# Block products for the feed-forward's output projection, on one Trainium2 core

## The chip, the core and the metric

The kernel runs on one core of a Trainium2 chip, in one launch. The metric is the device time of one execution in microseconds (us). TensorE multiplies matrices into psum; VectorE (DVE), ScalarE (ACT) and GpSimd (POOL) work element by element; SyncE (SP) issues all the transfers that matter here. VectorE and ScalarE read psum, POOL works on SBUF tiles alone.

## What is computed

The reference is one layer of a decoder trunk on 1024 prompt rows and 8 sample rows: a feed-forward, a token-mixing block, cross-attention, a second feed-forward, each with a residual and a LayerNorm. The change concerns the two feed-forwards alone:

```python
D_MODEL, D_FF = 1024, 2816
DN_ALPHA = (2.0 * DEPTH) ** 0.25          # DEPTH = 1

def _swiglu(h, wi, wo):
    u = h @ wi
    gate, up = u[..., :D_FF], u[..., D_FF:]
    return (jax.nn.silu(gate) * up) @ wo

h = _layer_norm(DN_ALPHA * h + 0.5 * _swiglu(h, P['ffn1_wi'], P['ffn1_wo']), P['ln_g'][0], P['ln_b'][0])
...
h = _layer_norm(DN_ALPHA * h + 0.5 * _swiglu(h, P['ffn2_wi'], P['ffn2_wo']), P['ln_g'][3], P['ln_b'][3])
```

All values are float32.

## The kernel before

Activations lie transposed: channels on the 128 partitions, the NT = 1032 rows along the free dimension. `S.acc` holds the 8 channel tiles of the residual stream. Every matrix product takes both operands as a high part and a low part (`split`: ScalarE rounds the high part, VectorE subtracts it for the low one) and runs three matmuls per tile, high by high, high by low, low by high (`mm3`, L125 to L127). `S.HH` and `S.HL` hold the two parts of 8 tiles of activations.

A feed-forward (`ffn`) has two stages. In the first, the hidden values silu(gate) times up are made, 22 tiles of 128 channels. Two tiles go as plain products (`classic`), the other 20 as 10 pairs (`pair`), in which the gate projection and then the up projection of two tiles are each made as seven block products in Winograd's form of Strassen's scheme: `left` loads four blocks of weights into raw tiles, forms their sums on POOL (L334) and yields the seven left factors B11, B21, T1, B22, T2, T3, T4 in this order; the right factors were made at the start (`UpForms`). HN = NT/4 = 258 is the width of one block of columns, p = 0, 1 are the halves of the rows. The hidden values of a pair, `G[m][p]`, go to a DRAM tensor `HID` (L407).

In the second stage the 22 hidden tiles come back in eight groups (`groups`, `loads`): 258-KB loads of HID and 256-KB loads of `wo` into raw tiles, each split in two. For each group, each of 8 output blocks m and each of the three column ranges CH3 (344 columns), `down_tile` sums the group's products in psum; ScalarE writes the first group's result to `S.acc` (L440), VectorE adds the others (L442). The residual `src` is added to `S.acc` on POOL between the groups (L464). The last group goes range by range, with the sums that LayerNorm needs (`ln_stat_step`).

LayerNorm is a stream of 20 steps (`ln_stream`): mean (L169), subtraction (L181), squares (L183), their sums over the partitions (L176), a power on POOL (L193), transposes that spread it (L200), scaling (L205), bias (L207), and, where another block follows, the two parts in HH and HL. `weave` interleaves such streams step by step as the program is written, so that of several streams the one with the smallest share done goes next; a second entry of a pair says how many steps a stream counts as. `settled` holds a stream back until the norm of the columns that it needs has been written. Norms that are pending at the end of a block are woven into the start of the next one.

The program is written with a scheduling layer that sets the order on each engine when it is built; on the chip each engine runs its list in that order. psum tiles of the feed-forward come from 6 banks, in the first stage from 8; the norms have two of their own in the second. Raw tiles: 7. Pairs of weight tiles: 7 in the first stage.

Of the kernel before, what the change touches and what calls it, by code (L numbers as in the profile page):

```python
# [19 lines left out]
NT = NP + NS  # L20
# [115 lines left out]
def ln_stat_step(S, st, m, c0, n):  # L136
# [23 lines left out]
def ln_stream(S, st, li, c0, n, final, keep):  # L160
# [11 lines left out]
    adds = nc.gpsimd if final is None or c0 + n < NT else nc.vector  # L172
# [6 lines left out]
    for k in range(KT):  # L179
        d = acc[:, k, c0:c0 + n]  # L180
        nc.vector.tensor_tensor(out=d, in0=d, in1=mu[:, :n], op=ALU.subtract)  # L181
        sq.append(S.lnp.tile([128, S.lnw], F32, tag="lnq", name="lnq", bufs=3))
# [39 lines left out]
LN_STEPS = 20  # L222

# [59 lines left out]
def ffn(S, octx, wi, wo, li, src, pre=(), final=None, keep=None, after=None):  # L283
# [5 lines left out]

    nc, tc = S.nc, S.tc  # L290
    HID = S.dram.tile([JT, 128, NT], F32, name="HID%d" % li)
    with ExitStack() as ctx:
# [39 lines left out]
        gt = pool(uctx, "fg", 6)  # L332
        TT = lambda o, a, b, op: nc.vector.tensor_tensor(out=o, in0=a, in1=b, op=op)
# [30 lines left out]
        def pair(j):  # L364
# [46 lines left out]
        groups = [[0, 1]] + [[3 * g + i for i in (2, 3, 4)] for g in range(5)] + [[17, 18], [19, 20, 21]]  # L411
        hd, wt = {}, {}
        S.hlseq = itertools.cycle([S.whl] * 2 + [S.hlx] * 2)

        def loads(js, to=None):
            for j in js:
                hd[j] = to() if to else (S.HH[:, j % KT, :], S.HL[:, j % KT, :])
                for p in range(2):
                    N = slice(2 * HN * p, 2 * HN * p + 2 * HN)
                    x = raw_tile(S)  # L420
                    nc.sync.dma_start(out=x, in_=HID[j, :, N])
                    split(nc, [t[:, N] for t in hd[j]], x)
                wt[j] = load_split(S, wo[128 * j:128 * j + 128, :])

        loads(groups[0])
        uctx.close()
        S.norms = Norms(S, octx, 344)
        hlast = pool(ctx, "fhl", 3)
        xw = pool(ctx, "fwo", 5)
        S.hlseq = itertools.cycle([S.hlx] * 2 + [xw] * 2 + [S.whl] * 3 + [xw] * 3 + [S.hlx] * 2)  # L430

        def down_tile(js, m, ni, st=None):
            c0, n = CH3[ni]
            q = psum(n)
            for j in js:
                hh, hl = hd[j]
                mm3(nc, q, wblock(wt[j], m), hh[:, c0:c0 + n], hl[:, c0:c0 + n], j == js[0], j == js[-1])
            a = S.acc[:, m, c0:c0 + n]
            if js[0] == 0:
                nc.scalar.activation(out=a, in_=q, func=AF.Identity, scale=0.5 / ALPHA)  # L440
            else:
                nc.vector.scalar_tensor_tensor(out=a, in0=q, scalar=0.5 / ALPHA, in1=a, op0=ALU.mult, op1=ALU.add)  # L442
            if st is not None:
                ln_stat_step(S, st, m, c0, n)

        def down_last(js, ni, st):
            for m in range(KT):
                down_tile(js, m, ni, st)
                yield

        banks = itertools.cycle([ps])
        last = lambda: [hlast.tile([128, NT], F32R, tag="h" + x, name="h" + x) for x in "hl"]
        for g, js in enumerate(groups[:-1]):
            loads(groups[g + 1], last if g + 2 == len(groups) else None)
            for m in range(KT):
# [1287 lines left out]
```

## Time and profile before

| | us |
|---|---|
| median of 3 executions | 3201.08 (3195.89 to 3203.86) |
| the profiled execution | 3202.45 |
| its span in the profile | 3200.7 |
| TensorE busy | 3015.8 |
| VectorE busy | 2198.6 |
| ScalarE busy | 1434.0 |
| POOL busy | 558.1 |

An engine's busy time is the union of its instructions. The records of neighbouring matmuls overlap, so the time that one costs is read from how many start in a stretch, not from its record. A wait is put down to what came last by the profile. Of the stages, the first feed-forward lies between 0 and about 724 us, the token mixing and attention between that and about 2448 us, the second feed-forward behind.

### The profile page before, as it was taken

The page shows a single profiled execution, that of the slowest core. Times are in us where ns is not written, and L with a number is a line of the kernel's source. Part 1 is how long each engine was busy: PE and PEld are TensorE (multiplying, and loading weights), DVE is VectorE, ACT ScalarE, POOL GpSimd, SP SyncE. Part 2 cuts the span into 40 slices and gives each one's busy share as a digit, 9 for nine tenths or more (in the row PEclk, how much of TensorE's full clock was granted, in tenths as well). Part 3 has the DMA queues.
Part 4 walks back from the last instruction along what each step waited for, and adds up shares of the span by engine and source line. Part 5 has one row for each costly group of instructions (what it writes and reads, how often), then busy time and mean ns, then how long its engine had stood idle before and what let it go on. Part 6 is the DMA issues. An engine that isn't in the chain of part 4 may idle for free. (4 is left out here: it accounts for less than half of the span.)

```text
span 3200.7 us, 63254 instructions
## 1 busy us (share of the span) xinstructions
PE 3015.8 (94%) x23324; PEld 2848.3 (89%) x23324; DVE 2198.6 (69%) x5903; ACT 1434.0 (45%) x3195; POOL 558.1 (17%) x526
## 2 busy tenths in 40 slices
PE   8999999999999999999999979889897999999997
PEld 8999999999888888888878858778887999999997
DVE  7666665574366887777777877776678666666556
ACT  5333352125465565556455655364235433334212
POOL 2222200132010011010001000260005322220111
PEclk9999999999999999999998969899999999999998
DMA  4222253314644554545554455554543222225321
GB/s 138 80 80 78 79 162 107 111 48 140 205 126 132 148 145 137 137 126 155 138 146 115 129 140 153 172 181 128 153 120 125 71 80 80 80 80 159 107 86 54
DMA packets 391301, 386.72 MB, mean 121 GB/s; under 512 B 153904, under 2 KB 292176, under 8 KB 390992
## 3 DMA queue, kind: packets, MB, share of 16 engines
q1 hardware_dynamic: 390992, 382.69, 40.4%
q8 instruction: 183, 3.00, 0.4%
q14 instruction: 126, 1.03, 0.1%
HBM read 277.54 MB, written 105.23 MB: 120 GB/s over the span
## 5 line engine op out<-in xcount | busy, mean ns | idle before, releaser
L125 PE MATMUL ps<-HH,wh 128*128 128x258 f32 (+1 forms) x2384 | 718.6, 302 | 18.7 <-ACT HH L510 7.8
L126 PE MATMUL ps<-HL,wh 128*128 128x258 f32 (+1 forms) x2384 | 716.7, 301 | 0.0
L127 PE MATMUL ps<-HH,wl 128*128 128x258 f32 (+1 forms) x2384 | 715.7, 300 | 0.0
L125 PE MATMUL g<-HH,wh 128*128 128x344 f32 (+2 forms) x1840 | 624.5, 340 | 15.9 <-DVE ql L1435 4.2
L127 PE MATMUL g<-HH,wl 128*128 128x344 f32 (+2 forms) x1840 | 596.8, 325 | 1.0 <-DVE wl L100 1.0
L126 PE MATMUL g<-HL,wh 128*128 128x344 f32 (+2 forms) x1840 | 594.3, 324 | 0.6 <-POOL HL L215 0.4
L125 PEld LDWEIGHTS ps<-HH,wh 128*128 128x128 f32 x2384 | 451.4, 189 | 21.0 <-ACT HH L510 7.8
L126 PEld LDWEIGHTS ps<-HL,wh 128*128 128x128 f32 x2384 | 451.2, 189 | 0.4 <-DVE HL L511 0.3
L127 PEld LDWEIGHTS ps<-HH,wl 128*128 128x128 f32 x2384 | 450.4, 189 | 0.0
L125 PEld LDWEIGHTS g<-HH,wh 128*128 128x128 f32 x1840 | 357.1, 194 | 35.3 <-DVE ql L1435 5.5
L126 PEld LDWEIGHTS g<-HL,wh 128*128 128x128 f32 x1840 | 357.7, 195 | 5.3 <-POOL HL L215 1.4
L127 PEld LDWEIGHTS g<-HH,wl 128*128 128x128 f32 x1840 | 356.1, 194 | 5.1 <-DVE wl L100 1.3
L228 ACT ACTIVATE wh<-raw 128x512 fp32r<-128x512 f32 x280 | 176.4, 631 | 322.2 <-PE ps L126 262.7
L334 POOL TENSOR_TENSOR raw<-raw 128x512 f32<-128x512 f32 x160 | 214.0, 1337 | 566.6 <-DVE wl L229 383.2
L229 DVE TENSOR_TENSOR wl<-raw,wh 128x512 fp32r<-128x512 f32 x280 | 206.7, 739 | 138.6 <-ACT wh L228 131.8
L100 DVE TENSOR_TENSOR wl<-raw,wh 128x512 fp32r<-128x512 f32 x302 | 218.6, 731 | 100.6 <-ACT wh L99 98.3
L99 ACT ACTIVATE wh<-raw 128x512 fp32r<-128x512 f32 x302 | 184.6, 625 | 222.5 <-PE ps L126 76.0
L442 DVE SCALAR_TENSOR_TENSOR acc<-ps,acc 128x344 f32<-128x344 f32 x336 | 168.4, 512 | 141.1 <-PE ps L127 140.4
L551 DVE TENSOR_TENSOR pr<-tq,iv 128x2 f32<-128x2 f32 (+30 forms) x496 | 160.8, 324 | 3.2
L556 ACT ACTIVATE ev<-g 128x344 f32<-128x344 f32 x192 | 86.9, 453 | 136.8 <-PE g L127 132.0
L949 DVE TENSOR_REDUCE tq<-pr 128x1 f32<-128x2 f32 (+30 forms) x496 | 121.8, 246 | 2.9
L556 ACT ACT_TABLE_LOAD x93 | 119.3, 1283 | 6.9 <-DVE cs L551 2.9
(404 smaller groups left out, 6302.8 us busy)
## 6 DMA issues: line engine op xcount, KB each, us to landing
raw<-in_wi_dram SPq DMA_DIRECT2D x176, 256.0 KB, 2.9
raw<-in_w_in_dram SPq DMA_DIRECT2D x116, 256.0 KB, 3.2
GD<-ev SPq DMA_DIRECT2D x168, 172.0 KB, 1.9
raw<-in_wo_dram SPq DMA_DIRECT2D x104, 256.0 KB, 2.8
raw<-HID SPq DMA_DIRECT2D x88, 258.0 KB, 3.6
HID<-g SPq DMA_DIRECT2D x80, 258.0 KB, 2.3
tg<-GD SPq DMA_DIRECT2D x32, 512.0 KB, 4.0
wt<-T SPq DMA_DIRECT2D x160, 64.0 KB, 2.9
```

What stands on the lines that cost most here:

```text
L99: nc.scalar.activation(out=hi, in_=raw, func=AF.Identity)
L100: S.low.tensor_tensor(out=lo, in0=raw, in1=hi.bitcast(F32), op=ALU.subtract)
L125: nc.tensor.matmul(ps, wh, xh, start=first, stop=False)
L126: nc.tensor.matmul(ps, wh, xl, start=False, stop=False)
L127: nc.tensor.matmul(ps, wl, xh, start=False, stop=last)
L228: nc.scalar.activation(out=hi, in_=x, func=AF.Identity)
L229: nc.vector.tensor_tensor(out=lo, in0=x, in1=hi.bitcast(F32), op=ALU.subtract)
L334: pool_tt = lambda o, a, b, op: nc.gpsimd.tensor_tensor(out=o, in0=a, in1=b, op=op)
L442: nc.vector.scalar_tensor_tensor(out=a, in0=q, scalar=0.5 / ALPHA, in1=a, op0=ALU.mult, op1=ALU.add)
L551: TTo = lambda o, a, b, op: nc.vector.tensor_tensor(out=o, in0=a, in1=b, op=op)
L556: ACT = lambda o, a, f=AF.Identity, **kw: nc.scalar.activation(out=o, in_=a, func=f, **kw)
L949: nc.vector.tensor_reduce(out=tq[:, 0:m, i], in_=pv, axis=mybir.AxisListType.X, op=ALU.add)
```

## The change

The output projection is made as seven block products as well. The 22 hidden tiles are taken as 11 pairs, rows of the product's inner dimension, so that each pair gives blocks (b11, b12; b21, b22) of hidden values, 128 channels by 258 columns for each half p, and of `wo`, 128 channels by 512 output columns. For each of seven forms and each half p, four output blocks are summed in psum over all 11 pairs and then added to `S.acc`, with the signs and partial sums of the scheme.

- In the first stage each pair now also makes its sums of hidden blocks (`hidden`: four subtractions of 258 columns per half on POOL, seven blocks written to DRAM `HF`) and of `wo` blocks (`sums`: four loads, four operations on 512 columns on POOL, four stores to DRAM `WF`). The two tiles made as plain products go by way of HID into such a pair, number 0, behind the first of the others.
- In the second stage form f's hidden blocks are loaded and split (`hid_prep`), its weights likewise (`w_prep`). While half 0 of form f runs, the hidden blocks of form f+1 are prepared; while half 1 runs, its weights. HH and HL hold the blocks of one form in the columns of one kind (b·1) and of the next form in those of the other kind, with extra tiles for pairs 8 to 10. There are 13 pairs of weight tiles.
- `S.acc` is loaded with the residual itself, by DMA; the POOL additions of it go.
- The last two forms finish columns 258 to 516, 774 to 1032, 0 to 258 and 516 to 774 in this order, so LayerNorm runs in four ranges of 258 columns in place of three of 344. The last half product goes block by block.
- `first_of` counts a norm's 20 steps as 80 where it is handed on: between the feed-forward's last half products, into the token mixing, into attention and into the second feed-forward.

The core of the diff:

```diff
@@ ln_stat_step, ln_stream, Norms @@
-        st.s = S.lnp.tile([128, S.lnw], F32, tag="lns", name="lns")[:, :n]
+        st.s = S.lnp.tile([128, 264], F32, tag="lns", name="lns", bufs=S.lnsums)[:, :n]
...
-    adds = nc.gpsimd if final is None or c0 + n < NT else nc.vector
+    adds = nc.gpsimd if final is None or c0 != 2 * HN else nc.vector
...
+def first_of(norm):
+    return norm[0], 4 * norm[1]
@@ ffn, first stage @@
-            for m in range(2):
-                for p in range(2):
-                    nc.sync.dma_start(out=HID[j + m, :, 2 * HN * p:2 * HN * p + 2 * HN], in_=G[m][p])
+            hidden(j // 2, G)
+
+        def hidden(i, G):
+            T = [ft.tile([128, 2 * HN], F32, tag="t%d" % t, name="t%d" % t) for t in range(4)]
+            sub = lambda o, a, b: pool_tt(o, a, b, ALU.subtract)
+            for p in range(2):
+                (b11, b12), (b21, b22) = ((g[p][:, :HN], g[p][:, HN:]) for g in G)
+                N = slice(HN * p, HN * p + HN)
+                t1, t2, t3, t4 = (t[:, N] for t in T)
+                for f, b in ((0, b11), (1, b21), (3, b22)):
+                    nc.sync.dma_start(out=HF[i, f, :, N], in_=b)
+                sub(t1, b12, b11)
+                sub(t3, b22, b12)
+                sub(t2, b22, t1)
+                sub(t4, t2, b21)
+            for f, t in zip((2, 4, 5, 6), T):
+                nc.sync.dma_start(out=HF[i, f], in_=t)
...
+        def sums(i):
+            t = [ft.tile([128, 512], F32, tag="w%d" % x, name="w%d" % x) for x in range(5)]
+            for x, b in zip(t, ((0, 0), (0, 1), (1, 1), (1, 0))):
+                nc.sync.dma_start(out=x, in_=weight(i, *b))
+            a11, a21, a22, a12, s1 = t
+            pool_tt(s1, a21, a22, ALU.add)
+            pool_tt(a21, a11, a21, ALU.subtract)
+            pool_tt(a11, a22, a21, ALU.subtract)
+            pool_tt(a12, a12, a11, ALU.subtract)
+            for n, x in enumerate((s1, a11, a21, a12)):
+                nc.sync.dma_start(out=WF[i, n], in_=x)
@@ ffn, second stage: groups, loads, down_tile, down_last and the POOL additions go @@
+        def hid_prep(f, k):
+            x = raw_tile(S)
+            nc.sync.dma_start(out=x, in_=HF[k, f])
...
+            split(nc, to, x.rearrange("q (p n) -> q p n", p=2))
+            HX[f, k] = to
+
+        def w_prep(f, k):
+            src = (weight(k, 0, 0), weight(k, 1, 0), WF[k, 0], WF[k, 3], WF[k, 1], WF[k, 2], weight(k, 1, 1))[f]
+            x = raw_tile(S)[:, :512]
+            nc.sync.dma_start(out=x, in_=src)
...
+            split(nc, W[f, k], x)
+
+        def add(f, q, m, p):
...
+            onto = lambda o, s=sc: nc.vector.scalar_tensor_tensor(out=o, in0=q, scalar=s, in1=o, op0=ALU.mult,
+                                                                 op1=ALU.add)
+            if form == "B11":
+                nc.scalar.activation(out=u, in_=q, func=AF.Identity, scale=sc)
+                pool_tt(c11, c11, u, ALU.add)
+            elif form == "B21":
+                onto(c11)
+            elif form == "T1":
+                onto(c12)
+                onto(c22)
+            elif form == "B22":
+                onto(c12)
+            elif form == "T2":
+                onto(u)
+                pool_tt(c12, c12, u, ALU.add)
+            elif form == "T3":
+                onto(u)
+                TT(c22, c22, u, ALU.add)
+                pool_tt(c21, c21, u, ALU.add)
+            else:
+                onto(c21, -sc)
+
+        def one_pass(f, p, st=None):
...
+            qs = [psum(HN) for _ in range(4)]
+            for k in range(NJ):
+                if f < 6:
+                    (w_prep if p else hid_prep)(f + 1, k)
+                for m in range(4):
+                    step(m, k, qs[m])
+                yield
+            for m in range(4):
+                result(m, qs[m])
+
+        for k in range(KT):
+            hid_prep(0, k)
+            if k < 7:
+                w_prep(0, k)
         uctx.close()
...
+        for k in range(KT):
+            nc.sync.dma_start(out=S.acc[:, k, :], in_=src[k])
+        pre = []
+        for f, p in itertools.product(range(7), range(2)):
+            st = SimpleNamespace() if f > 4 else None
+            weave((one_pass(f, p, st), NJ), *pre)
+            if (f, p) == (6, 0) and after is not None:
+                ahead(S, after)
             if st is not None:
+                pre = [first_of((ln_finish(S, st, li, 2 * HN * p + HN * (6 - f), HN, final, keep), LN_STEPS))]
     return pre
@@ mixer, attention @@
-        return [norm(3)]
+        return [first_of(norm(3))]
```

## Rows read from the trace of the kernel before

**Rows 1.** The page's first part: busy time, share of the span, instructions.

```profile
PE 3015.8 (94%) x23324; PEld 2848.3 (89%) x23324; DVE 2198.6 (69%) x5903; ACT 1434.0 (45%) x3195; POOL 558.1 (17%) x526
```

**Rows 2.** Stretches: length, each engine's busy time (instructions), granted clock, DMA share, GB/s.

```profile
57.00:460.00 403.00, 403.00 (x3361) 403.00 (x3360) 272.91 (x511) 152.98 (x316) 101.46 (x76) 1.00 0.27 86
500.00:600.00 100.00, 100.00 (x635) 100.00 (x634) 59.25 (x106) 20.63 (x35) 10.86 (x8) 1.00 0.37 112
724.00:732.00 8.00, 4.80 (x15) 4.33 (x16) 6.08 (x16) 7.66 (x18) 6.14 (x7) 0.59 0.72 256
2467.00:2495.00 28.00, 20.76 (x114) 20.04 (x114) 20.45 (x40) 14.67 (x38) 16.02 (x17) 0.82 0.21 71
2510.00:2913.00 403.00, 403.00 (x3361) 403.00 (x3361) 270.53 (x502) 150.86 (x309) 100.41 (x76) 1.00 0.27 85
2913.00:3175.00 262.00, 258.14 (x1643) 256.04 (x1641) 155.59 (x294) 63.30 (x121) 33.37 (x29) 1.00 0.31 96
3175.00:3200.70 25.70, 8.54 (x32) 6.57 (x32) 15.52 (x35) 10.84 (x22) 0.85 (x1) 0.59 0.31 110
2900.00:2925.00 25.00, 23.17 (x174) 22.88 (x173) 19.84 (x41) 15.78 (x34) 0.00 (x0) 1.00 0.81 254
```

**Rows 3.** Matmuls of the tiles T4 and hh: durations ns, first and last start.

```profile
L127 PE MATMUL ps<-T4h,wl x8: 281/283/287, 457.2 to 459.8; 128*128 128x258 f32 x8
L127 PE MATMUL ps<-hh,wl x72: 313/320/406, 678.0 to 723.4; 128*128 128x344 f32 x72
L127 PE MATMUL ps<-T4h,wl x160: 281/283/287, 2527.7 to 2913.1; 128*128 128x258 f32 x160
L127 PE MATMUL ps<-hh,wl x72: 313/320/404, 3131.4 to 3174.0; 128*128 128x344 f32 x72
```

**Rows 4.** ScalarE's groups by line, 445 to 467 us: count, busy us, mean ns, idle.

```profile
L228 ACT ACTIVATE HH<-raw 128x516 fp32r<-128x516 f32 x12 | 7.4, 632 | 7.3 <-DMA raw<-HID 7.2
L99 ACT ACTIVATE wh<-raw 128x512 fp32r<-128x512 f32 x8 | 4.9, 625 | 3.5 <-issue 2.0 <-DMA raw<-in_wo_dram 1.5
```

**Rows 5.** Groups by line and shape, whole span: count, busy us, mean ns, idle.

```profile
L334 POOL TENSOR_TENSOR raw<-raw 128x512 f32<-128x512 f32 x160 | 214.0, 1337 | 566.6 <-DVE wl L229 383.2 <-DMA raw<-in_wi_dram 75.3 <-issue 56.5
L229 DVE TENSOR_TENSOR HL<-raw,HH 128x516 fp32r<-128x516 f32 x76 | 54.6, 734 | 34.6 <-ACT HH L228 34.5
L333 DVE TENSOR_TENSOR p<-p,ps 128x258 f32<-128x258 f32 x80 | 33.9, 424 | 46.4 <-PE ps L127 41.1
L181 DVE TENSOR_TENSOR acc<-acc,ln 128x344 f32<-128x344 f32 x48 | 22.4, 504 | 2.5 <-PE ln L169 2.3
L181 DVE TENSOR_TENSOR acc<-acc,ln 128x256 f32<-128x256 f32 x48 | 18.2, 411 | 1.2 <-PE ln L169 1.2
```

**Rows 6.** Instructions of LayerNorm in order of time: start us, duration us.

```profile
2434.34 0.59 PE L169 MATMUL ln<-lns,ones_d 128*128 128x256 f32 x2
2443.87 0.44 PE L200 MATMUL ln<-ident,lnx 128*128 128x128 f32 x2 [1.49 <-ACT lnx L195]
2450.34 1.08 PE L169 MATMUL ln<-lns,ones_d 128*128 128x264 f32 x2
2474.36 0.90 PE L200 MATMUL ln<-ident,lnx 128*128 128x128 f32 x3 [1.75 <-ACT lnx L195]
3180.13 1.48 PE L169 MATMUL ln<-lns,ones_d 128*128 128x344 f32 x2 [4.42 <-DVE lns L145]
3197.13 0.58 ACT L207 ACTIVATE acc<-acc,lnb 128x344 f32<-128x344 f32 x1 [0.21 <-DVE acc L205]
```

**Rows 7.** Line 246's POOL subtractions: durations ns min/median/max, first and last start.

```profile
L246 POOL TENSOR_TENSOR acc<-acc x16: 730/860/1320, 22.9 to 2492.4; 128x258 f32<-128x258 f32 x16
```

**Rows 8.** VectorE and POOL in order of time, 403.9 to 406.3 us: start, duration.

```profile
403.93 1.29 POOL L334 TENSOR_TENSOR raw<-raw 128x512 f32<-128x512 f32 x1 [5.70 <-DVE wl L229]
404.40 1.10 DVE L333 TENSOR_TENSOR g<-g,c 128x258 f32<-128x258 f32 x1
405.91 0.43 DVE L333 TENSOR_TENSOR g<-g,c 128x258 f32<-128x258 f32 x1
```

More of the change, by code (lines that the diff above doesn't have):

```diff
@@ L409, in ffn @@
         for j in range(2, JT, 2):
             pair(j)
[L411 to L423, printed above, removed]
@@ L425, in ffn @@
-        loads(groups[0])
-        uctx.close()
[L427 to L442, printed above, removed]
-            if st is not None:
-                ln_stat_step(S, st, m, c0, n)
@@ L446, in down_last @@
[L446 to L455, printed above, removed]
-                for ni in range(3):
-                    down_tile(js, m, ni)
-            if 2 <= g < 6:
-                for k in (2 * g - 4, 2 * g - 3):
-                    for p in range(2):
-                        a = S.acc[:, k, 2 * HN * p:2 * HN * p + 2 * HN]
-                        x = raw_tile(S)
-                        nc.sync.dma_start(out=x, in_=src[k, :, 2 * HN * p:2 * HN * p + 2 * HN])
-                        nc.gpsimd.tensor_tensor(out=a, in0=a, in1=x, op=ALU.add)
@@ L465, in ffn @@
-        if after is not None:
-            ahead(S, after)
-        pre = []
-        for ni in range(3):
-            st = SimpleNamespace()
-            weave((down_last(groups[-1], ni, st), KT), *pre)
-            pre = [(ln_finish(S, st, li, *CH3[ni], final, keep), LN_STEPS)]
+            sums(j // 2)
+            if j == 2:
+                G = [[gt.tile([128, 2 * HN], F32, tag="g%d" % m, name="g", bufs=3) for _ in range(2)] for m in range(2)]
+                for m, p in itertools.product(range(2), range(2)):
+                    nc.sync.dma_start(out=G[m][p], in_=HID[m, :, 2 * HN * p:2 * HN * p + 2 * HN])
+                hidden(0, G)
+                sums(0)
@@ new lines, in ffn @@
+        for k in range(KT):
+            hid_prep(0, k)
+            if k < 7:
+                w_prep(0, k)
+        uctx.close()
+        S.norms = Norms(S, octx, 2)
+        hx = pool(ctx, "fhx", 1)
+        room.hx = [[hx.tile([128, NJ - KT, 2, HN], F32R, name="hx%d%s" % (c, y)) for y in "hl"] for c in range(2)]
+        room.u = pool(ctx, "fu", 1).tile([128, 4, 2 * HN], F32, name="fu")
+        xw = pool(ctx, "fwo", 6)
+        S.hlseq = itertools.cycle([xw] * 6 + [S.hlx] * 4 + [S.whl] * 3)
@@ new lines, in ffn @@
+        for k in range(7, NJ):
+            if k >= KT:
+                hid_prep(0, k)
+            w_prep(0, k)
+        banks = itertools.cycle([ps])
+        for k in range(KT):
[6 more added lines that the diff above has]
+                ahead(S, after)
+            if st is not None:
+                pre = [first_of((ln_finish(S, st, li, 2 * HN * p + HN * (6 - f), HN, final, keep), LN_STEPS))]
@@ L519, with __init__ @@
 class Norms:
-    def __init__(self, S, ctx, width=264):
-        S.lnw = width
+    def __init__(self, S, ctx, sums=1):
+        S.lnsums = sums
         self.ctx = ctx.enter_context(ExitStack())
@@ L1620, in attention @@
             weave((attend(h), 44 if h < 3 else 50), (samples(h), 21), (fill(h), 49 if h < 3 else 40))
-        return [norm(3)]
+        return [first_of(norm(3))]
 @with_exitstack
```

44 lines of the change are left out of this document (42 added, 2 removed).

## The prediction

> **What bounds the kernel now.** I read the busy table first: TensorE is busy in 94% of the span [rows 1]. The stretches then show where it is not [rows 2]. In both feed-forwards the stage of the gate and up projections (57 to 460 us and 2510 to 2913 us) has TensorE busy throughout at the full granted clock, 1.00 of 2.4 GHz, and so has the output stage behind it, almost: in 2913 to 3175 us 258.1 of 262 us. VectorE is busy 68% and 59% there, the DMA engines 27% and 31%. So a change of the output stage is worth what it takes off TensorE's stream, as long as nothing else becomes late. The places where TensorE does stand are the two restarts (724 to 732 us behind the first feed-forward, 2467 to 2495 us at the head of the second) and the end (3175 to 3200.7 us), where it is busy 8.5 of 25.7 us.
>
> **The main term: matmuls.** The output stage now has 22 tiles x 8 blocks x 3 column ranges x 3 = 1584 matmuls of 344 columns; 635 start in 100 us [rows 2], so 0.1575 us each, 249.5 us in all. The change has 7 forms x 2 halves x 4 blocks x 11 pairs x 3 = 1848 matmuls of 258 columns. That shape runs in the gate and up stage, 3361 in 403 us [rows 2]: 0.1199 us each, so 221.6 us, 27.9 us less per feed-forward. That a matmul goes to another psum bank after every third is not shown there; I take no cost for it (bounds: 0 to 10 ns each, 18 us a stage).
>
> The Trainium skill, "TensorE: Matmul & The Clock Gate", section "Back-to-back issue gap", gives N/2.4 + 2.5 ns at full clock: by an estimate from it 1584 x 145.8 - 1848 x 110.0 = 27.6 us, as the rows have it. The same section also gives a sustained figure for LDWEIGHTS and MATMUL pairs, 81 ns at 128 columns and 131 ns at 512; on a line between them the 1848 would take 8 us more than the 1584. The rows' 119.9 and 157.5 ns speak for the first.
>
> **The output stage, term by term.** The first stage now runs from the last T4 matmul at 459.8 to the last one at 723.4 us [rows 3], 263.6 us. After: 221.6 us of matmuls, plus these.
> - LayerNorm inside the stage. From 678.0 to 723.4 us there are 214 of the last group's matmuls, 33.5 us at 0.1575, so two norms take 11.9 us of TensorE time, waits in; in the second feed-forward 3131.4 to 3174.0 us leaves 9.1 us [rows 3]. That is 4.5 to 5.9 us each. After, three norms of 258 columns lie inside instead of two of 344; at 4.7 us each, 14 us.
> - The head of the first product. From 459.8 to 678.0 us the 1371 matmuls would take 215.9 us, so 2.3 us are lost now [rows 3]. After, the first half product needs 22 blocks loaded and split, two for each 1.44 us step of TensorE. Around the same place 20 blocks are split in 22 us now [rows 4], 1.1 us each. Room for B11 in HH is free when B21 of the last pair has run, five forms of 24 matmuls ahead, 14.4 us; with the 15.8 us of the half product that is 30.2 us for 22 x 1.1 = 24.2 us. So it nearly hides; I take 3 us (bounds 0 to 12, as the last pair's sums and the 4 MB of acc go over the same queue).
> - Bank turnover. Four of six banks are filled at once; the third block of the next half product needs the bank of the first one before, whose last matmul is 9 back and whose next use 6 ahead, 1.8 us. VectorE may have a split of 0.73 us running and then reads psum in 0.42 us pieces [rows 5], twice per block for T1: 1.6 us for the first block, 2.4 us for the second against 2.2. I take 2 us a stage (bounds 0 and 12 handovers of 1 us).
> - VectorE and ScalarE: 154 splits in place of 88, 154 x 0.73 = 113 us, and some 30 us of evictions, beside 240 us; the stage's cover is wide. The 16 additions of the residual on POOL go; acc is loaded instead.
>
> Sum 221.6 + 14 + 3 + 2 = 240.6 us, so 23.0 us less in the first feed-forward. Behind it, 724 to 732 us holds 15 matmuls where the full rate gives 51 [rows 2]: 5.7 us lost. After, the first range of the mixer waits for one eviction only, but the second range (344 to 688) needs the last norm (516 to 774) with one range of four projections, 15 us, as cover. I take 3 us lost, a gain of 2.7.
>
> In the second feed-forward 2913.1 to 3200.7 us is 287.6 us [rows 2, 3]. The end now takes 6.1 us from the last matmul (3174.0) to the last norm's first (3180.1; VectorE is still at the norm before), 17.6 us from there to the last activation's end, 3 us for the store [rows 3, 6]. After, the norm before it has a whole half product of 15.8 us to finish, so I take 1.5 us; the norm's pieces shrink as its subtractions do, 504 ns at 344 columns to 411 at 256 [rows 5], so 14.6 us; the store stays 3: 19 us. 240.6 + 19 = 259.6, a gain of 28.0 us.
>
> **The gate and up stage.** Each pair of 40.3 us gets 8 subtractions of 258 columns and 4 of 512 on POOL, at 0.86 and 1.34 us [rows 5, 7] 12.2 us, and 14 more DMAs, 2.9 MB. POOL is busy 10.1 us per pair now, VectorE 27.3 us [rows 2]. A subtraction of two SBUF operands took VectorE 1.10 us beside a running POOL one of 1.29 us, and 0.43 us alone [rows 8]: the added POOL time costs VectorE about half of itself, 6 us per pair, 33.4 of 40.3 us. At worst all of it: 39.5. Queued behind a late POOL operation are, on SP, the T stores and behind them the next weight loads; they have most of a projection as slack. I take 4 us for both stages (bounds 0 to 40, 2 us a pair).
>
> The Trainium skill, "SBUF — State Buffer", section "Who interferes with whom", says that a VectorE instruction with two SBUF inputs contends with a GpSimd instruction that reads SBUF; the trace agrees with 1.10 us against 0.43. If the lock were whole each time, by that page the 39.5 us above would hold and the sum would be some 20 us worse.
>
> **The order of the norms.** Three entries now give the pending norm the first quarter of the woven work. At the head of the second feed-forward a norm takes 24.0 us from its mean to its transposes (2450.3 to 2474.4), the one before it 9.5 us (2434.3 to 2443.9) [rows 6]. TensorE waits for it: 2467 to 2495 us holds 114 matmuls where 178 would fit, 10.1 us lost, partly at half clock (0.82 on average) [rows 2]. At 9.5 us the norm is there 14 us sooner, ahead of the range that needs it. I take 8 us gained (bounds -3, if the forms it now passes are late in its place, and 10). The entry to attention shows no such loss; 0.
>
> **Sum.** -23.0 - 2.7 - 28.0 - 8 + 4 = -57.7 us from the profiled execution's 3202.45 us (span 3200.7): 3145 us. The median of the runs is 3201.08, 1.4 us below that execution; I leave it.
>
> **Rivals.**
> - The small costs nearly vanish: heads and banks at 0, the up stage at 0, the entry at -10: 3145 - 10 - 4 - 2 = 3129 us. For it: TensorE's slack in the up stage. Chance 0.10.
> - POOL's added work reaches TensorE in the up stage, 2 us in each of 20 pairs: 3145 + 36 = 3181. It decides once VectorE nears the 40.3 us of a pair; 33.4 is my figure and 39.5 the bound. Chance 0.12.
> - The head and the banks cost what their bounds say, 9 and 10 us more in each stage: 3183. For it: DMA at 0.81 and 254 GB/s around the present head [rows 2]. Chance 0.12.
> - Slower: block loads set the pace. The stage moves 154 blocks of 0.26 MB and 4 MB of acc, 186 GB/s, where now 112 GB/s take a share of 0.37 [rows 2], so some 0.6. They decide above 221.6/154 = 1.44 us a block, and make the kernel slower than before above about 1.63. With seven raw buffers that is 11 us for a buffer to be filled, split and freed. At 1.85 us a block each stage takes 63 us more: 3272. Against it: 1.1 us [rows 4]. Chance 0.07.
> - A matmul's interval does not fall with the columns, 0.1575 us for both: 1848 x 0.1575 = 291 us, 69 us more per stage, 3284. Against it: 3361 of this very shape. Chance 0.02. The sustained figure in the Trainium skill's "TensorE: Matmul & The Clock Gate", "Back-to-back issue gap", points this way.
>
> **How the numbers follow.** The forecast, 3145 us (own range 3129 to 3165), has 0.55; the rivals 0.10, 0.12, 0.12, 0.07 and 0.02, and 0.02 are left to something unseen. A measurement of this kernel can tell 0.3%, 9.6 us. Slower: 0.07 + 0.02 + 0.01 = 0.10; within: 0.03, from the two 3180 cases falling together; faster: 0.87. The range from 3126 to 3188 us takes in all but the slow cases and those pairs.
>
> **What would show it.** Right: some 1848 matmuls of 258 columns at 0.120 us between the last T4 of the pairs and the last product, in about 241 us; no wait of TensorE above 1 us inside the pairs; VectorE near 33 us a pair; the norm at the head of the second feed-forward some 10 us from mean to transposes; 19 us from the last matmul to the end. Wrong: waits of TensorE for splits or for evictions at the starts of half products, clocks below 1.00 in either stage, or DMA shares above 0.8 through the output stage.

## The result, and the profile after

The changed kernel takes 3245.55 us (median of 4 executions, 3237.11 to 3246.39) beside 3201.75 for the kernel before: a ratio of 1.0134, 95% interval 1.0118 to 1.015. It is slower, by 43.8 us, where 3145 us was forecast. The profiled execution is the one of 3237.11 us (span 3235.3); why the other three are 9 us longer is not settled.

The first part of the page of after, to be read beside [rows 1]:

```profile
PE 2995.9 (93%) x23910; PEld 2821.4 (87%) x23910; DVE 2254.3 (70%) x5875; ACT 1494.7 (46%) x3335; POOL 839.9 (26%) x826
```

TensorE is busy 20 us less than before, yet the span is 34.6 us longer: time went into standing. Stretches of after, columns as in [rows 2] (length, busy time and instructions of PE, PEld, DVE, ACT, POOL, then granted clock, DMA share, GB/s):

```profile
57.00:100.00 43.00, 42.76 (x357) 42.55 (x355) 24.74 (x42) 15.01 (x37) 27.77 (x20) 1.00 0.71 230
100.00:200.00 100.00, 80.26 (x587) 78.49 (x588) 60.62 (x94) 24.49 (x58) 71.28 (x62) 0.88 0.69 223
200.00:300.00 100.00, 96.45 (x788) 95.85 (x787) 76.19 (x130) 30.42 (x69) 59.87 (x53) 0.98 0.44 144
300.00:460.00 160.00, 160.00 (x1336) 160.00 (x1335) 117.31 (x199) 56.90 (x120) 69.81 (x64) 1.00 0.31 97
...
497.00:540.00 43.00, 41.77 (x343) 41.15 (x343) 27.24 (x40) 21.99 (x41) 11.03 (x13) 1.00 0.93 318
540.00:681.00 141.00, 136.52 (x1129) 135.06 (x1128) 85.92 (x153) 60.20 (x99) 9.94 (x13) 1.00 0.61 190
...
2600.00:2700.00 100.00, 85.63 (x655) 84.44 (x655) 64.52 (x94) 23.89 (x56) 74.55 (x60) 0.91 0.65 217
2700.00:2961.00 261.00, 261.00 (x2178) 261.00 (x2177) 195.57 (x340) 98.32 (x208) 109.00 (x99) 1.00 0.35 111
```

A full 100 us holds 836 matmuls of 258 columns. The gate and up stage has that rate from 300 us on, with its hidden blocks still being subtracted, and loses 249 matmuls (30 us) between 100 and 200 us. There TensorE stands for 19.7 us; in the 80.26 us that it is busy its matmuls take 0.137 us each, at a mean granted clock of 0.88 (part of the time at 1.2 instead of 2.4 GHz), which is 10 us more. The second feed-forward does the same at 2544 to 2700 us. What fills that stretch is POOL, 71.28 of 100 us, and the transfers. The tiles that bound the stages, as in [rows 3], and the tile of the weight sums (durations, first and last start):

```profile
L127 PE MATMUL ps<-T4h,wl x160: 278/283/419, 73.9 to 495.3; 128*128 128x258 f32 x160
L127 PE MATMUL ps<-hx0h,wl x96: 277/283/419, 507.2 to 751.3; 128*128 128x258 f32 x96
...
L127 PE MATMUL ps<-T4h,wl x160: 281/283/419, 2544.0 to 2961.5; 128*128 128x258 f32 x160
L127 PE MATMUL ps<-hx0h,wl x96: 277/282/292, 2973.4 to 3215.7; 128*128 128x258 f32 x96
...
L345 POOL TENSOR_TENSOR w<-w,w x44: 1261/1302/1745, 66.4 to 219.0; 128x512 f32<-128x512 f32 x44
```

All 44 operations of the weight sums run between 66 and 219 us, though the program calls `sums` once behind each of the 10 pairs (and once more behind the first, for pair 0). The waits of after from 57 to 460 us (who waited, for what: us in all, times, longest):

```profile
...
DVE wl L234 <- ACT wh L233: 85.7, 49, 11.1
ACT wh L233 <- POOL raw L345: 72.3, 10, 12.3
...
POOL w L345 <- DMA w<-in_wo_dram: 31.3, 8, 6.0
POOL raw L345 <- DMA raw<-in_wi_dram: 14.6, 2, 7.6
...
PE ps L125 <- DVE u L344: 14.2, 6, 7.7
...
PE ps L125 <- DVE g L344: 5.6, 2, 2.8
PE ps L125 <- DVE c L344: 3.7, 4, 1.5
...
SPq L450 <- POOL w L345: 73.4, 36, 5.5
```

Read upwards from TensorE: it waits for psum that VectorE has not emptied, VectorE (which takes its list in order) for the high part of a weight factor, ScalarE for a sum of gate or up weights that POOL has not made yet, and POOL has the sums of `wo` in front of it in its list, some of them waiting for their loads. A piece of that, in order of time (start, duration; in brackets the wait before it; `w` are sums of `wo`, `raw` those of gate or up weights):

```profile
134.51 6.27 POOL L345 TENSOR_TENSOR w<-w,w 128x512 f32<-128x512 f32 x4 [6.02 <-DMA w<-in_wo_dram]
140.75 2.90 POOL L345 TENSOR_TENSOR raw<-raw 128x512 f32<-128x512 f32 x2
146.81 5.38 POOL L345 TENSOR_TENSOR w<-w,w 128x512 f32<-128x512 f32 x4 [3.16 <-DMA w<-in_wo_dram]
152.15 2.62 POOL L345 TENSOR_TENSOR raw<-raw 128x512 f32<-128x512 f32 x2
154.80 2.19 ACT L233 ACTIVATE wh<-raw 128x512 fp32r<-128x512 f32 x4 [11.65 <-POOL raw L345]
```

### The profile page after: what moved, and what is told of

Read it like the earlier page. It is cut to its first block, busy times and chain, and to the rows that moved or that the text cites. A ratio compares the mean times of both kernels' runs of the same rounds, so it can differ in the third digit from the quotient of the medians.

```text
span 3235.3 us, 65790 instructions
## 1 busy us (share of the span) xinstructions
PE 2995.9 (93%) x23910; PEld 2821.4 (87%) x23910; DVE 2254.3 (70%) x5875; ACT 1494.7 (46%) x3335; POOL 839.9 (26%) x826
## 5 line engine op out<-in xcount | busy, mean ns | idle before, releaser
L125 PE MATMUL ps<-HH,wh 128*128 128x258 f32 (+1 forms) x2368 | 692.1, 292 | 58.4 <-DVE u L344 25.9
L127 PE MATMUL ps<-HH,wl 128*128 128x258 f32 (+1 forms) x2368 | 685.2, 289 | 0.4 <-DVE wl L234 0.4
L126 PE MATMUL ps<-HL,wh 128*128 128x258 f32 (+1 forms) x2368 | 684.8, 289 | 0.1
L234 DVE TENSOR_TENSOR wl<-raw,wh 128x512 fp32r<-128x512 f32 x434 | 370.2, 864 | 222.3 <-ACT wh L233 215.3
L233 ACT ACTIVATE wh<-raw 128x512 fp32r<-128x512 f32 x434 | 269.1, 627 | 484.0 <-PE ps L126 279.4
L100 DVE TENSOR_TENSOR wl<-raw,wh 128x512 fp32r<-128x512 f32 x214 | 154.7, 730 | 84.7 <-ACT wh L99 83.8
L99 ACT ACTIVATE wh<-raw 128x512 fp32r<-128x512 f32 x214 | 132.2, 626 | 87.0 <-PE g L126 18.4
L385 ACT ACTIVATE g<-g 128x258 f32<-128x258 f32 x160 | 66.5, 415 | 219.6 <-DVE g L344 206.4
L345 POOL TENSOR_TENSOR w<-w,w 128x512 f32<-128x512 f32 x88 | 122.4, 1391 | 87.1 <-DMA w<-in_wo_dram 68.5
L901 POOL TENSOR_TENSOR ivc<-ivc,mhalf 128x4 f32<-128x4 f32 x32 | 32.7, 1023 | 394.2 <-DVE ivc L657 325.8
## 6 DMA issues: line engine op xcount, KB each, us to landing
raw<-in_wi_dram SPq DMA_DIRECT2D x176, 256.0 KB, 3.0
raw<-in_w_in_dram SPq DMA_DIRECT2D x116, 256.0 KB, 3.5
w<-in_wo_dram SPq DMA_DIRECT2D x88, 256.0 KB, 4.4
WF<-w SPq DMA_DIRECT2D x88, 256.0 KB, 2.1
raw<-WF SPq DMA_DIRECT2D x88, 256.0 KB, 3.7
```

Source lines behind the costliest of these rows:

```text
L99: nc.scalar.activation(out=hi, in_=raw, func=AF.Identity)
L100: S.low.tensor_tensor(out=lo, in0=raw, in1=hi.bitcast(F32), op=ALU.subtract)
L125: nc.tensor.matmul(ps, wh, xh, start=first, stop=False)
L126: nc.tensor.matmul(ps, wh, xl, start=False, stop=False)
L127: nc.tensor.matmul(ps, wl, xh, start=False, stop=last)
L233: nc.scalar.activation(out=hi, in_=x, func=AF.Identity)
```

## The stages of every run

"Up" is the first T4 matmul of the pairs to the last, "down" from there to the last matmul of the output stage, "mid" from there to the first T4 of the second feed-forward, "tail" from the last product to the end of the span; profiled executions, us. The ratio is that of the medians to the kernel before on the same chip.

| run | up 1 | down 1 | mid | up 2 | down 2 | tail | ratio (95%) |
|---|---|---|---|---|---|---|---|
| before | 385.5 | 263.6 | 1804.3 | 385.4 | 260.9 | 26.7 | 1 |
| after | 421.4 | 256.0 | 1792.7 | 417.5 | 254.2 | 19.6 | 1.0134 (1.0118 to 1.015) |
| e1_no_sums | 385.4 | 263.4 | 1791.4 | 385.4 | 254.3 | 19.6 | 0.9939 (0.9921 to 0.9956) |
| e2_paced | 391.5 | 271.9 | 1799.9 | 392.2 | 268.5 | 20.5 | 1.0047 (1.003 to 1.0064) |
| e3_norms_plain | 422.0 | 255.4 | 1793.5 | 417.3 | 251.9 | 20.7 | 1.0135 (1.0118 to 1.0153) |
| e4_before_sums | 414.9 | 263.9 | 1801.6 | 409.7 | 260.4 | 27.6 | 1.0175 (1.016 to 1.019) |
| e5_shift | 401.4 | 256.2 | 1790.2 | 399.7 | 251.8 | 20.0 | 0.9992 (0.998 to 1.0003) |
| e6_norm_late | 421.1 | 249.8 | 1795.6 | 417.4 | 252.9 | 19.8 | 1.0101 (1.0074 to 1.0128) |
| e7_acc_late | 419.7 | 262.4 | 1793.7 | 418.5 | 256.6 | 20.0 | 1.0137 (1.0115 to 1.016) |
| f1_paced_all | 398.3 | 252.2 | 1801.6 | 399.3 | 252.2 | 20.0 | 0.999 (0.9978 to 1.0002) |
| g1_moves_only | 392.7 | 256.0 | 1797.2 | 386.1 | 253.8 | 20.1 | 0.9945 (0.9926 to 0.9963) |
| g2_ops_only | 424.4 | 258.1 | 1794.3 | 421.5 | 254.3 | 20.3 | 1.0158 (1.0135 to 1.018) |
| f2_spread_late | 401.9 | 259.1 | 1799.3 | 400.6 | 256.1 | 21.0 | 1.0018 (1.0006 to 1.003) |
| f3_one_ahead | 393.6 | 261.2 | 1799.1 | 394.1 | 258.7 | 20.3 | 0.9986 (0.9972 to 1.0) |
| f4_three_ahead | 398.9 | 252.5 | 1797.8 | 394.4 | 251.6 | 20.4 | 0.9985 (0.9972 to 0.9998) |
| f5_two_ahead | 399.3 | 249.6 | 1803.4 | 395.0 | 250.1 | 20.4 | 0.9986 (0.9975 to 0.9997) |
| f6_four_g | 390.9 | 253.4 | 1798.6 | 387.8 | 251.4 | 20.7 | 0.9939 (0.9926 to 0.9952) |
| f7_four_g_spread | 391.9 | 257.7 | 1797.0 | 390.2 | 263.1 | 20.4 | 1.0004 (0.9995 to 1.0013) |
| h1_changed_four_g | 430.4 | 256.4 | 1797.6 | 430.9 | 254.2 | 20.4 | 1.0228 (1.0205 to 1.025) |

## The experiments

The two theories of the up stage: the *place* of the sums in lists that are taken in order (called A in the expectations), against the *amount* of work that POOL does beside VectorE (B).

**Leave the sums of weights out.**

```diff
-            sums(j // 2)
-                sums(0)
-            src = (weight(k, 0, 0), weight(k, 1, 0), WF[k, 0], WF[k, 3], WF[k, 1], WF[k, 2], ...)[f]
+            src = (weight(k, 0, 0), weight(k, 1, 0), weight(k, 0, 1), weight(k, 0, 0), ...)[f]
```

> The changed kernel without the sums of wo blocks: their 44 POOL operations, 44 loads and 44 stores per feed-forward go, and the second stage loads plain wo blocks in place of the sums, as many bytes as before (the sums are left out of what is computed). In the changed kernel's trace the gate and up stage takes 421.4 and 417.5 us from its first to its last T4 matmul, where the kernel before took 385.5 and 385.4. Theory A (the sums depend on nothing in the pairs, all 11 stand early in POOL's and SP's lists, wait there for their own loads, and the next projections' POOL sums and weight loads wait behind them): both stages back to 386 to 390 us, whole kernel about 3180 us. Theory B (what costs is the amount of added POOL work and what it does to VectorE, wherever it stands): the sums are 5.3 of 12.2 us added per pair, so less than half of the loss goes: stages of about 404 us, kernel about 3215 us.

Up comes to 385.4 us in both feed-forwards, that of the kernel before. All 88 subtractions of hidden blocks per feed-forward are still there. Stretches of this run:

```profile
100.00:200.00 100.00, 100.00 (x836) 100.00 (x835) 72.55 (x125) 36.18 (x78) 52.06 (x49) 1.00 0.37 119
200.00:300.00 100.00, 100.00 (x836) 100.00 (x836) 72.45 (x124) 34.41 (x72) 43.28 (x40) 1.00 0.29 94
```

POOL is busy 52 of 100 us and TensorE loses nothing. The hidden blocks cost nothing; the sums cost all.

**The same sums, paced by sharing tiles with the pair's hidden blocks** (so that set k cannot load before the stores of pair k have left):

```diff
-            t = [ft.tile([128, 512], F32, tag="w%d" % x, name="w%d" % x) for x in range(5)]
+            t = [ft.tile([128, 2 * HN], F32, tag="t%d" % x, name="w%d" % x)[:, :512] for x in range(4)]
+            t.append(ft.tile([128, 512], F32, tag="w4", name="w4"))
```

> The changed kernel with all its work; only the four tiles into which the wo blocks are loaded share their slots with the four tiles of hidden sums, so that the sums of weights of pair i can stand only between the hidden sums of pair i and of the next one: one set per pair in POOL's list in place of eleven sets in the first half. Theory A: the gate and up stages fall to 386 to 392 us and the kernel to about 3180 us, as without the sums. Theory B: the same work costs the same, stages of about 418 us, kernel within 10 us of 3245.

```profile
100.00:200.00 100.00, 95.74 (x785) 95.53 (x785) 74.85 (x115) 32.24 (x71) 69.10 (x61) 0.98 0.57 185
200.00:300.00 100.00, 100.00 (x836) 100.00 (x836) 82.08 (x124) 35.38 (x77) 57.08 (x47) 1.00 0.45 149
300.00:460.00 160.00, 160.00 (x1337) 160.00 (x1336) 131.02 (x203) 58.05 (x125) 89.61 (x76) 1.00 0.50 164
...
480.00:520.00 40.00, 31.07 (x199) 29.56 (x199) 16.33 (x21) 14.72 (x30) 12.05 (x12) 0.79 0.84 299
```

From 57 to 460 us POOL works 232.1 us, 3.4 more than in the changed kernel, and up falls from 421.4 to 391.5: place, not amount. The first line says the same of one stretch: POOL is about as busy from 100 to 200 us as in the changed kernel (69.10 against 71.28 us), and TensorE runs 785 matmuls there in place of 587. The last line is the price at the other end: the eleventh set stands behind the last pair, meets the loads of the output stage, and down grows by 16 and 14 us (E in the expectations).

**The old output stage with the sums beside it** (their result used by nothing):

```diff
@@ in before.py, ffn @@
             pair(j)
+            sums(j // 2)
```

> The kernel before, with the sums of wo blocks alone added in the gate and up stage as the change has them (loads, four POOL operations, stores to DRAM for each of 11 pairs; nothing reads them). Theory A: the stage lengthens by 20 to 35 us in each feed-forward, kernel 3245 to 3270 us. Theory B: 5.3 us of POOL work a pair costs less than half of what the change cost, 10 to 15 us a stage, kernel 3222 to 3232 us.

Up 414.9 and 409.7: 29 and 24 us for the sums alone, without any of the rest.

**Their transfers alone, and their operations alone.**

```diff
@@ moves only @@
-            pool_tt(s1, a21, a22, ALU.add)          (and the other three)
@@ operations only: five tiles loaded once @@
-            for x, b in zip(t, ((0, 0), (0, 1), (1, 1), (1, 0))):
-                nc.sync.dma_start(out=x, in_=weight(i, *b))
...
-                nc.sync.dma_start(out=WF[i, n], in_=x)
```

> The weight sums' 44 loads and 44 stores per feed-forward stay where they are, their POOL operations are left out (what is stored to WF is the plain blocks, so the output is not the reference's). If it is SyncE's list and the traffic that cost the up stage (the loads and stores in front of the next weight loads), most of the 36 and 32 us above the stages of E1 (385.4 us) stay: above 410 us each, and the whole at about 3245. If it needs POOL's waits for the loads, with the next projection's sums behind them, the up stages fall to 386 to 395 us and the whole to about 3185. I lean to the second, 0.65.

> The weight sums' POOL operations stay, 44 per feed-forward at the same places in POOL's list, on five tiles loaded once, with no loads and stores of their own (the weight factors of the output stage are plain blocks, so the output is not the reference's). If POOL's 59 us of work in the first half of the stage delays the next sums by itself, the up stages stay above 405 us. If what costs is that POOL stands waiting for their loads, the up stages come to 386 to 392 us and the whole to about 3185.

The transfers alone cost 7 us in the first stage and 1 in the second. The operations alone cost 39 and 36, against what I leaned to: no load has to be late. (Three of the four write another tile there, and nothing reads the results.) They do not stand quite where they stood, though. Freed of loads, they were put still closer, and from 100 to 150 us, where POOL is busy 45.5 of 50 us, TensorE runs 136 of 419 matmuls. POOL in order of time in that run (start, us, operation, count):

```profile
93.67 13.79 POOL L345 TENSOR_TENSOR w<-w,w 128x512 f32<-128x512 f32 x10
107.41 1.26 POOL L345 TENSOR_TENSOR raw<-raw 128x512 f32<-128x512 f32 x1
108.63 1.26 POOL L345 TENSOR_TENSOR w<-w,w 128x512 f32<-128x512 f32 x1
109.86 1.73 POOL L345 TENSOR_TENSOR raw<-raw 128x512 f32<-128x512 f32 x1
111.55 10.71 POOL L345 TENSOR_TENSOR w<-w,w 128x512 f32<-128x512 f32 x8
```

Between two sums that a projection needs (`raw`) stand up to ten that no product of the stage needs. So this run shows that POOL's early work is enough; how much of the changed kernel's 36 us its 31.3 us of waits for loads add is not separated.

**Where the sets may stand.** Of the paced kernel, the set at the end is moved:

```diff
+            for i in {1: [1], 2: [0, 2], 3: [3, 4], 4: [5], ..., 9: [10], 10: []}[j // 2]:
+                sums(i)
```

> The paced kernel, but with the sums of the last pair's weights made one pair earlier (two sets of sums behind the second and the third pair, none behind the last). In the paced kernel the gate and up stage lost only 6 us, but the output stage took 271.9 and 268.5 us where the changed kernel takes 256.0 and 254.2. Theory E (the last set of sums came behind the last pair, held the room that the output stage's tiles, weights and acc take over, and put their loads on top of each other): output stage back to 256 and 254 us, stages of pairs 388 to 395, kernel about 3190. Rival F (with the pairs 29 us shorter the loads of the first product have less time, wherever the sums stand): output stage stays near 268 us, kernel about 3215.

Down returns to 256 and 252, but up is 401.4 and 399.7: one more pair with two sets behind it costs some 8 us there. Two other plans, both with the norms of the output stage later (the edit e6 below):

> The sums one set behind each pair, two behind pairs 6 and 9, none behind the last one, and the norms inside the output stage three steps of the last products later. If a doubled set costs what it did behind pairs 2 and 3 (7 us each), up 398 and 398, down 250 and 252, the whole at about 3195, no better than before. If those two doubled sets cost for standing at the stage's start, where the pair 0 is made too, up 388 and 388 and the whole at about 3178.

> As the run before it, but one set stands ahead of the first pair, so only pair 9 has two. If the doubled sets cost 7 us each, up 392 and the whole at about 3185; if a set at the head of the stage delays the first weights of the pairs, the time goes to the stretch ahead of the first T4 product and the whole to about 3195.

In the up stage the first case of each held: a doubled set costs about 8 us behind late pairs too (f2 against f3: one of them less, up 8 and 7 us less), and one set ahead of the first pair is free (361 matmuls in 57 to 100 us, as before). What stayed was a loss of about 7 us at 100 to 150 us, 362 and 361 of 419 matmuls. The whole times, 3211.7 and 3201.8 us, missed that first case by some 17 us: down stayed at 256 to 261 where 250 to 252 was expected. It is 250 to 253 in the next two runs, which have no doubled set behind pair 9, so that set is probably paid there. Three or two sets ahead, with the place of pair 0's blocks free or taken:

> Three sets of weight sums stand ahead of the first pair, none behind pair 1 (where the hidden blocks of pair 0 are made too), one behind each of pairs 2 to 9, none behind the last; the norms in the output stage as in the run with one set ahead. If a set costs TensorE nothing wherever POOL's list has no other added work beside it, the stretch 100 to 150 us is full (419 matmuls), the up stages come to 386 to 390 us and the whole to about 3186, 0.5% under the kernel before. If three sets ahead delay the pairs' own sums as in the changed kernel (three sets stand in its first 50 us too), the up stages stay at 394 or more and the whole at about 3200.

> As the run with three ahead, but two stand ahead of the first pair and one behind pair 1, beside the blocks of pair 0. If it is the meeting with pair 0's blocks that costs the 7 us at 100 to 150 us, they stay: up 393, the whole at about 3193. If not, up 387 and the whole at about 3185.

Neither removed it: 331 and 303 of 419 matmuls from 100 to 150 us. The waits of the run with two ahead, 80 to 150 us:

```profile
PE ps L125 <- DVE g L344: 11.2, 1, 11.2
...
DVE g L344 <- DMA WF<-w: 9.5, 1, 9.5
```

VectorE cannot write a `g` tile. Three buffers of each are there, and a pair takes two; those of pair 0 stay taken until POOL has subtracted and SyncE has stored, and SyncE's stores of `HF` stand behind stores of `WF` that wait for POOL. SyncE's list in that run, ahead of the next write of `g` at 123.40 us:

```profile
117.40 4.34 SPq L451 DMA_DIRECT2D WF<-w  x4
121.84 0.90 SPq L427 DMA_DIRECT2D HF<-g  x2
```

A fourth buffer:

```diff
-  tag="g%d" % m, name="g", bufs=3)
+  tag="g%d" % m, name="g", bufs=4)
```

> The kernel with two sets ahead, with four buffers of each g tile in place of three. In the run with two ahead VectorE stood 9.5 us at 114 to 123 us before it could write a g tile, and TensorE 11.2 us behind it. If the g tiles that the pair 0 and its subtractions hold are the cause, that wait goes, 100 to 150 us holds 419 matmuls, up comes to 386 to 388 us in both and the whole to about 3180. If POOL's place in the list is the cause, up stays above 393 us and the whole at about 3194.

> The kernel with sets spread late (two behind pairs 6 and 9), with four buffers of each g tile. If a doubled set costs its 7 us by holding g tiles, the up stages fall from 402 and 401 to 388 and the whole to about 3185. If it costs by its place in POOL's list ahead of the next pair's sums, they stay above 396 and the whole at about 3205.

Up falls by 8.4 and 7.2 us in the first, by 10.0 and 10.4 in the second. In the second, 100 to 150 us is full (419 matmuls in place of 362); its end of the stage (1293 of 1336 matmuls from 300 to 460 us) and down 2 at 263.1 still lose, and its whole time, 3202.27 us, is that of the kernel before and not the 3185 expected. The first is the best version found: 3180.83 us, 0.6% under the kernel before and some 2% under the changed one. It has paced sums, two sets ahead of the first pair and none behind the last, the later norms and four buffers. From 100 to 150 us it has

```profile
100.00:150.00 50.00, 47.97 (x387) 47.76 (x386) 36.15 (x58) 14.23 (x33) 34.10 (x31) 0.97 0.48 149
```

387 matmuls instead of 303, though not the 419 expected. Is the buffer, then, the cause in the changed kernel?

> The changed kernel with four buffers of each g tile in place of three, and nothing paced: the sets of weight sums still stand early in POOL's list, two or so in every projection (for room, the tile of the first sum is 504 columns wide, and its last 8 columns are stored from the plain block, so the output is not the reference's). If the place of the sums in POOL's list costs by itself, the up stages stay above 410 us and the whole above 3225. If it cost only because the g tiles stayed taken until POOL had subtracted, the up stages come to 386 to 395 us and the whole to about 3190. Between the two, in proportion. I lean to the first, 0.6.

No. With four buffers and the sums left early, up is 430.4 and 430.9, more than before the edit:

```profile
100.00:150.00 50.00, 38.57 (x290) 38.16 (x289) 25.59 (x38) 10.87 (x26) 35.74 (x34) 0.86 0.54 184
150.00:200.00 50.00, 40.43 (x303) 40.01 (x302) 27.16 (x46) 12.14 (x28) 31.31 (x27) 0.86 0.62 205
200.00:250.00 50.00, 38.34 (x290) 37.54 (x289) 24.97 (x45) 9.84 (x22) 32.19 (x28) 0.90 0.65 213
```

The early place costs by itself; the fourth buffer pays only once the sums are paced. (This run also makes 11 small stores more per feed-forward, for the columns left out of the first sum; what they add is not separated.)

**The output stage.** Its loss against the forecast stands mostly at the norms. TensorE's waits in after, 480 to 760 us:

```profile
PE ln L169 <- DVE lns L145: 6.7, 2, 4.2
PE ps L125 <- DVE acc L492: 2.5, 4, 0.8
PE ln L169 <- issue: 2.2, 1, 2.2
PE ln L200 <- ACT lnx L195: 2.0, 3, 0.7
PE ps L125 <- DVE fu L492: 1.4, 1, 1.4
```

Three edits: the norms there at an even pace, the norms three steps of the products later, and the upper four tiles of acc loaded later:

```diff
@@ e3: inside the output stage, but for the last half product @@
-  pre = [first_of((ln_finish(...), LN_STEPS))]
+  pre = [(ln_finish(...), LN_STEPS)]
@@ e6 @@
+  pre = [(itertools.chain(itertools.repeat(None, 22), pre[0][0]), pre[0][1])]
@@ e7: before the half product (1, 0) @@
+  for k in range(4, KT): nc.sync.dma_start(out=S.acc[:, k, :], in_=src[k])
```

> The changed kernel, but inside the output stage the norms are woven into the next half product at an even pace, no longer in its first quarter; the three entries stay. Theory C (TensorE, whose list is fixed, stands at the norm's mean and transposes because they were put ahead of where their inputs are ready; some 11 us of waits and 3 to 7 us at half clock per output stage): the output stage of the first feed-forward falls from 256 to about 246 us, the second's likewise, kernel 15 to 20 us faster, about 3228. Rival D (VectorE is what is late in the last four half products, whatever the order): no change beyond 5 us, or slower.

> The changed kernel; inside the output stage each norm enters the next half product some 3 of its 11 steps later (4.3 us). Theory C (TensorE's list has the norm's mean ahead of the moment at which VectorE has the sums ready; 8.9 us of such waits in the first and 4.6 us in the second output stage): the waits at the mean go, output stages 3 to 9 us shorter, kernel 8 to 15 us faster than 3245. Rival D (VectorE is late whatever TensorE's list says): the waits turn up at the later steps of the norm or at the products' own evictions, no change beyond 4 us.

> The changed kernel; the upper four tiles of acc (2.1 of 4.2 MB) are loaded at the third half product and not ahead of the first. In the changed kernel the DMA engines stand at 0.95 to 0.97 from 500 to 540 us, and 520 to 600 us holds 635 matmuls where 676 fit, 4.8 us lost. Theory G (the transfers at the head of the first product set the pace there): 2 to 5 us less in each output stage, kernel 4 to 10 us faster. Rival H (these are evictions that come late for the banks, not transfers): no change.

The even pace changes nothing that can be told. Later norms (C in the expectations) take 6.2 us off down 1 and 1.3 off down 2: the matmul of the mean, put into TensorE's list as soon as its product is written, stood waiting for VectorE's sums (6.7 us above). With the later norms that wait is 3.5 us. The later acc gains nothing (down 1 even 6.4 us longer), against G. But half of the 4.2 MB was moved, and the DMA engines were as busy at the head as before (0.95 from 500 to 540 us, 0.96 without the edit), so whether transfers or late evictions hold the head is not shown. (From 520 to 600 us the trace of after has 628 matmuls where 667 would fit, not 635 and 676; the loss named is the same.) The paced sums with none behind the last pair, the later norms and the later acc together:

> All three together: paced sums with none behind the last pair, norms some 3 steps later, upper tiles of acc later. Under theories A, C, E and G: pairs 388 to 395 us, output stages 245 to 250 us, kernel about 3175 us, faster than the kernel before by 0.8%. Under A and E alone: 3190 us. Under F: 3215 us.

3199.98 us, no faster than the kernel before: up is still 13 us longer in each feed-forward than without the sums, with the loss at 100 to 150 us (368 of 419 matmuls) and, behind the two doubled sets, from 200 to 300 us (787 of 836).

## Why the prediction was wrong, step by step

- **The gate and up stage is the step that failed.** Taken 4 us for both (bounds 0 to 40); measured 35.9 + 32.1 = 68.0, outside the bounds. The working spread the 4 operations of a set over each pair, "12.2 us" of POOL per pair, because the diff calls `sums` behind each pair. But nothing in `sums` depends on the pair, and the layer that orders the lists is free to put it early; it did, one set per 14 us instead of one per 40. The amount was right: POOL works 228.7 us from 57 to 460 us where it worked 101.5 [rows 2], 12.7 us more per pair. The sentence on what is queued behind a late POOL operation named the T stores and the next loads, and not the next sums of gate weights in POOL's own list, which is where TensorE's chain ran. The rival of this place, 2 us per pair (36 us in all), had POOL right and the mechanism wrong: VectorE was to be filled by contention.
- **Contention with POOL** was taken as half of POOL's added time. Over 57 to 460 us VectorE's busy time went from 272.9 [rows 2] to 291.8 without the sums, for 71.8 us more of POOL, and to 319.7 in the paced kernel, for 130.7 more: 0.26 and 0.36 of it. It stands in the operations with two SBUF operands, such as the low parts of the weights (the kernel before, then the paced one, 57 to 460 us; count, busy us, mean ns):

```profile
L229 DVE TENSOR_TENSOR wl<-raw,wh 128x512 fp32r<-128x512 f32 x137 | 100.9, 738 | 67.0 <-ACT wh L228 63.7
...
L234 DVE TENSOR_TENSOR wl<-raw,wh 128x512 fp32r<-128x512 f32 x140 | 143.3, 1030 | 47.9 <-ACT wh L233 45.8
```

Those that read one operand from psum did not change (`p<-p,ps`: 424 ns [rows 5], 419 in the paced kernel). These rows agree with the rule of the Trainium skill, "SBUF — State Buffer", "Who interferes with whom", that a VectorE instruction with two SBUF inputs contends with a GpSimd instruction that reads SBUF. TensorE loses nothing by it while VectorE has 18 of 100 us left, as the second and third lines of the paced kernel show.
- **The matmul term was right.** 1336 in 160 us are 0.1198 us each, and in the output stage 600 to 640 us holds 331 where 334 would fit.
- **The output stage was mis-sized:** 240.6 against 256.0 and 254.2, a gain of 7.6 and 6.7 us to the last product where 23.0 and 20.3 were forecast. Head and banks: 497 to 681 us holds 1472 matmuls, 176.5 us at 0.1199, so 7.5 us lost where 5 were taken. Norms: 366 of the 1848 remain for the 70.3 us behind 681, 43.9 us, so 26.4 us went to three norms with their handovers where 14 was taken. TensorE stands for 10.9 us of that stretch, and its mean granted clock is 0.95; before, in the stretch with two norms, it stood for 3.1 of 45.4 us at 1.00 (the kernel before, then after):

```profile
678.00:723.40 45.40, 42.35 (x274) 40.06 (x272) 32.22 (x67) 15.94 (x34) 20.04 (x21) 1.00 0.09 32
...
681.00:751.30 70.30, 59.38 (x452) 57.30 (x453) 49.36 (x125) 33.83 (x86) 36.50 (x49) 0.95 0.23 71
```

The price of 4.7 us was read from norms of 344 columns that followed a whole range; the new ones follow so close on their sums that TensorE waits for them, 6.7 us in the first feed-forward. The later norms showed a part of that. In the second feed-forward this wait is 1.3 us and the gain no larger, so what the norms pay for there stays open.
- **Mid was right as a sum, in part by luck:** -11.6 us against -2.7 - 8. From the mean of the pending norm to the first T4 of the second feed-forward it is 73.5 us now and was 77.4 [rows 3, 6], 3.9 us less where 8 was taken: that norm takes 18.1 us from its mean to its transposes, after 24.0 [rows 6], where some 10 were expected. The mixer's restart gave 3.3 us where 2.7 was taken: the mixer's first matmul into tile `m` starts 140.3 us behind the last product, and was at 143.6. The remaining 4.5 us or so lie between, from that matmul to the norm's mean, 1578.8 us after 1583.4, where the prediction took nothing for the entry to attention. In the other runs with block products, whose code there is the same, this stretch takes 1575.8 to 1589.6 us, so its part of the sum is luck.

The norm's rows of after, and those of the last one, in order of time:

```profile
2470.47 1.08 PE L169 MATMUL ln<-lns,ones_d 128*128 128x264 f32 x2
2488.54 0.56 PE L200 MATMUL ln<-ident,lnx 128*128 128x128 f32 x3 [0.56 <-ACT lnx L195]
...
3217.09 0.67 PE L169 MATMUL ln<-lns,ones_d 128*128 128x258 f32 x2 [1.07 <-DVE lns L145]
...
3230.82 1.17 ACT L207 ACTIVATE acc<-acc,lnb 128x258 f32<-128x258 f32 x2 [0.28 <-DVE acc L205]
```

- **The tail was right:** 19.6 us against 19: 1.4 us from the last product (3215.7) to the norm, 14.9 to its last activation's end, 3.3 for the store.
- **Of the slow rivals** none happened: the interval fell with the columns, and block loads did not set the pace (540 to 681 us runs 1129 matmuls in 141 us, with DMA at 0.61).

## What to carry to other kernels

Ask of every added operation what it depends on, not where it is called: here the scheduling layer put work that depends on nothing late early into a list that the critical work also uses, and a single buffer did not hold it back. Give such work a dependence that paces it (here: tiles shared with the step that it should follow), spread it one unit per step, and leave no unit behind the last step. A buffer count is worth trying again after the order is mended, not before: the same fourth buffer gave 8 us in one order and nothing in the other.

## What was not expected of the hardware

- With the sums' transfers alone in place, the DMA engines were busy 0.81 of the time at 258 GB/s from 100 to 200 us, and TensorE's pairs still ran 783 of 836 matmuls:

```profile
100.00:200.00 100.00, 94.70 (x783) 93.87 (x781) 51.65 (x104) 27.90 (x65) 41.52 (x42) 1.00 0.81 258
```

- A standing TensorE lost more than it stood: in the changed kernel's 100 to 200 us, 19.7 us idle came with 10 us of matmuls at the lower clock (0.88 in the mean).
